# Mixture of experts on one core: tokens turned ahead of the first product, the list of further blocks moved behind the last expert

## The chip, the core and the metric

The kernel runs on one core of a Trainium2 chip. Its engines are TensorE (PE; its weight loads are shown as PEld), VectorE (DVE), ScalarE (ACT), GpSimd (POOL) and SyncE (SP), each with an instruction stream of its own that runs in order; they wait for each other by semaphores. Sixteen DMA engines move data between HBM and the core's memory. POOL issues the indirect DMAs (gather of rows, scatter with addition); SP issues most others. The metric is the device time of one execution in microseconds, as a median over runs.

## What is computed

One block of a hybrid model on 2048 tokens of width 1024: a token mixer with four branches, then a mixture of 32 experts with two experts for each token, then a norm. Only the experts matter here:

```
def grouped_experts(h, expert_ids, weights, w1, w3, w2):
    # tokens sorted by expert, in blocks; for each block xb of expert e:
    #   out = (silu(xb @ w1[e]) * (xb @ w3[e])) @ w2[e]
    # then out * weight of the token for this expert, summed over the token's two experts

def hier_moe(...):
    # group by argmax of group logits, then the two best experts of the group
x = x + m_l[5] * y_l.reshape(x.shape)
return rms_norm(x, final_norm_w)
```

An expert has w1 and w3 of 1024x512 and w2 of 512x1024, in float32: 6.3 MB for each, and all 32 are read.

## The kernel before

The mixer and the router fill the first 2205 us or so. Then come the experts, one after another, and behind them the final norm. The change lies in `ffn`, in the part from line 796 on.

**One expert.** The router has left a list of token rows for each expert, up to 192 of them in two parts: a first block of 128, and a rest of up to 64 in two blocks of 32 that stand behind guards (`tc.If` on the expert's count). `gather` (line 846) fetches the rows with an indirect DMA into one of two tiles, `xg` of 128 rows or `xg` of 64 rows; there is one buffer of each, and the 1025th column of a row is the token's weight for this expert. `turn` (880) turns the 128 rows: eight transposes on PE in two halves of four, each half into a PSUM bank `ps_tr` (there are two such banks, which all transposes share), and `parts` (864) takes each half out as a rounded high part (`xh`, ScalarE cast, line 869) and the remainder (`xl`, VectorE, line 870). `turn` also copies the weight column into `w0` (884). `turn_rest` does it for the 64 rows, in full precision (`xq`, and four small copies into `w1`). `up` (895) is the first product: 48 matmuls with 512 columns, three for each pair of parts (lines 1368 to 1370), against w1 and w3, then silu on ScalarE (903) and the gate on VectorE (904), which multiplies by `w0`; its result `mh0` is turned like `xg` into `hh` and `hl`. `down` (918) is the second product with 24 matmuls, a product with `m5` on VectorE (921), and `added`, the scatter onto the rows of X1 in HBM (908), one tile `my0`. The rest blocks have the same steps in `up_rest`, `gate_rest` (`mh1`, turned into `hq`) and `down_rest`, and use 32-column tiles of PE.

**Weights.** `unit` (800) loads 512 KB into a tile `mraw` (pool of `RAW` = 16), then `split` makes the rounded part `mhi` (ScalarE cast, line 1224) and the remainder `mlo` (VectorE, line 1225), pools of `PARTS` = 12 each. An expert has twelve units: four each for w1, w3 and w2. The rest blocks read `mraw` itself.

**The loop** (from line 1018) writes, for expert e: `up_rest(e)`, the gate of the rest, `up(e)`, the turning of `mh1`, then `turn(e+1)` and `turn_rest(e+1)`, the two gathers of expert e+2, the weights w1 and w3 of e+1, `down(e-1)`, the weights w2 of e, `down_rest(e)` and the turning of `mh0`. A scheduler then sets the final order on each engine; what the program says is only its input. Buffers are freed and taken by semaphores between the engines.

**The list of further blocks.** `beyond` (972) works out on VectorE which experts have more than 192 tokens, as a list `ovt`, `ovf` for a loop behind all experts, whose count is read by `values_load`. It stands behind expert 4. Its tile `le` has the tag of `mh1` and so shares its one buffer.

**The end.** Behind the loop over further blocks, X1 is loaded in 16 tiles, some of which take over slots of `mraw` and the others slots of `mhi` and `mlo`; each is squared, normed and stored.

Of the kernel before, what the change touches and what calls it, by code (L numbers as in the profile page):

```python
# [4 lines left out]
F32 = mybir.dt.float32  # L5
F32R = mybir.dt.float32r
# [555 lines left out]
NE, FF = 32, 512  # L562
# [1 line left out]
NSLOT = 2  # L564
FIT = 192
NONE = 1 << 20
RAW, PARTS = 16, 12
OVB = 32


def ffn(tc, G, A, out, bcast, rsqrt, split, mm3, MT, MR, X1, FR, mid):
# [9 lines left out]
    hl = rp.tile([128, 2, 2, N], BF, name="hl")  # L581
# [23 lines left out]
    with tc.tile_pool(reuse_waits="tile", name="wo", bufs=1, side="right") as wop, \  # L605
# [5 lines left out]
        y0, w1 = [mid.part(0, k) for k in range(4)], mid.kept(1)  # L611
# [195 lines left out]
    wp = mo.enter_context(tc.tile_pool(reuse_waits="tile", name="mo", bufs=1))  # L807
# [39 lines left out]
    def gather(idx_ap, half, guard):  # L847
        xg = xgs[half]
        with guard():
            nc.gpsimd.indirect_dma_start(out=xg, out_offset=None, in_=FR,  # L850
                                         in_offset=bass.IndirectOffsetOnAxis(ap=idx_ap, axis=0),
                                         bounds_check=2 * T - 1, oob_is_err=False)
        return xg

    def turned_into(put, src, r, n, w=128):

        for c in range(0, n, 512 // r):
            m = min(n - c, 512 // r)
            pt = psum("tr")
            for k in range(m):  # L860
                nc.tensor.transpose(pt[:, k * r:(k + 1) * r], src[:, (c + k) * 128:(c + k + 1) * 128], G.ident[:r, :r])
            put(slice(c, c + m), pt[:, :m * r].rearrange("p (k t) -> p k t", t=r))

    def parts(src, n, name):

        hi, lo = (wp.tile([128, n, 128], F32R, name=name + c) for c in "hl")

        def put(c, v):
            nc.scalar.copy(hi[:, c], v)
            nc.vector.tensor_sub(lo[:, c], v, hi[:, c].bitcast(F32))  # L870
        turned_into(put, src, 128, n)
        return hi, lo

    def plain(src, n, name):

        t = wp.tile([128, n, 64], F32, name=name)
        turned_into(lambda c, v: nc.scalar.copy(t[:, c], v), src, 64, n)
        return t

    def turn(xg):  # L880

        p = parts(xg, 8, "x")
        w = wp.tile([128, 1], F32, name="w0", bufs=2)
        nc.scalar.copy(w, xg[:, D:D + 1])
        return p, w

    def turn_rest(xg):

        p = plain(xg, 8, "xq")
        w = wp.tile([64, 2], F32, name="w1", bufs=2)  # L890
        for j, h in product(range(2), range(2)):
            nc.scalar.copy(w[h * 32:h * 32 + 32, j:j + 1], xg[j * 32:j * 32 + 32, D:D + 1])
        return p, w

    def up(xw, w1, w3):

        x, w = xw
        pa = [psum("mm"), psum("mm")]
        for p, ws in zip(pa, (w1, w3)):
            mm3(p, lambda k: (x[0][:, k], x[1][:, k]),  # L900
                lambda k: tuple(t[:, (k % 2) * 512:(k % 2) * 512 + 512] for t in ws[k // 2][:2]), range(8))
        h = wp.tile([128, FF], F32, name="mh0")
        nc.scalar.activation(h, pa[0], AF.Silu)
        nc.vector.scalar_tensor_tensor(h, pa[1], w, h, op0=OP.mult, op1=OP.mult)
        return h
# [8 lines left out]
    def down(h, w2, dst, rest=()):  # L914

        y = wp.tile([128, D], F32, name="my0")
        py = [psum("sc"), psum("sc")]
        for c, (p, ws) in enumerate(zip(py, w2)):
            o = slice(512 * c, 512 * c + 512)
            mm3(p, lambda k: (h[0][:, k], h[1][:, k]), lambda k: tuple(t[:, o] for t in ws[k][:2]), range(4))  # L920
            nc.vector.tensor_mul(y[:, o], p, m5[:, o])  # L921
        added(y, dst, X1, rest)


    def quarters(p, n, guard, x, ws):

        def block(j):
            with guard(j):  # L928
                for k, g in product(range(n), range(4)):
                    nc.tensor.matmul(p[g * 32:g * 32 + 32, j * 256:j * 256 + 256], x(k, j), ws(k, g),  # L930
                                     start=k == 0, stop=k == n - 1)
                if not j:
                    block(1)
        block(0)

    def up_rest(xw, w1, w3, guard):

        w = [w1, w3]
        quarters(hu, 8, guard, lambda k, j: xw[0][:, k, j * 32:j * 32 + 32],
                 lambda k, g: w[g // 2][k // 2][2][:, (k % 2) * 512 + (g % 2) * 256:][:, 0:256])  # L940

    def gate_rest(xw):
        h = wp.tile([64, FF], F32, name="mh1")
        nc.scalar.activation(h, hu[0:64], AF.Silu)
        for j in range(2):
            o = slice(j * 256, j * 256 + 256)
            nc.vector.scalar_tensor_tensor(h[:, o], h[:, o], xw[1][:, j:j + 1], hu[64:128, o], op0=OP.mult, op1=OP.mult)
        return h
# [17 lines left out]
    def in_weights(e_, q=nc.sync, eng=lambda n, u: nc.vector):  # L966
        f2 = lambda n, u: A[n][e_][:, 2 * u:2 * u + 2].rearrange("p k n -> p (k n)")
        return [[unit(f2(n, u), q, eng(n, u)) for u in range(4)] for n in ("e1", "e3")]
# [33 lines left out]
    def fetch(e_, guard):  # L1002
        return gather(idx[:, e_:e_ + 1], 0, nullcontext), gather(idx[0:64, NE + e_:NE + e_ + 1], 1, guard)
# [3 lines left out]
    over = lambda big: lambda j: tc.If(big > 128 + 32 * j)  # L1007
    guards = [over(load(e_)) for e_ in range(2)]
    rows_ = fetch(0, nullcontext)
    x = turn(rows_[0]), turn_rest(rows_[1])  # L1010
    rows_ = fetch(1, lambda: guards[1](0))
    sct4 = wr.tile([128, NE, 2], I32, name="sct4")
    for g, j in product(range(4), range(2)):
        nc.gpsimd.tensor_scalar(sct4[g * 32:g * 32 + 32, :, j], sct[j * 32:j * 32 + 32, NE:], 4.0, float(g), op0=OP.mult, op1=OP.add)
    with tc.issue_after(listed.ins):
        w13 = in_weights(0, eng=lambda n, u: nc.gpsimd if n == "e1" and u < 2 else nc.vector)
    last = None
    for e_ in range(NE + 1):
        if e_ < NE:
            guard = guards[e_]  # L1020
            if e_ + 2 < NE:
                guards.append(over(load(e_ + 2)))

            up_rest(x[1], *w13, guard)
            h1 = gate_rest(x[1])
            h = up(x[0], *w13)
            t1 = plain(h1, 4, "hq")
            q = nc.sync if e_ else nc.gpsimd
            if e_ + 1 < NE:
                x = turn(rows_[0]), turn_rest(rows_[1])  # L1030
                if e_ + 2 < NE:
                    rows_ = fetch(e_ + 2, lambda: guards[e_ + 2](0))
                w13 = in_weights(e_ + 1, q)
        if last:
            down(last[0], [last[1]] * 2, sct[:, e_ - 1:e_], last[2])
        if e_ < NE:
            w2 = [unit(A["e2"][e_][:, u], q) for u in range(4)]
            rest = down_rest(t1, w2, guard, e_)
            last = parts(h, 4, "h"), w2, rest
            if e_ == 4:  # L1040
                beyond()


# [8 lines left out]
    with tc.For_i(0, nov, 1) as it:  # L1052
        ee = nc.values_load(ovt[0:1, bass.ds(it, 1)], min_val=0, max_val=NE - 1)
        sb = wp.tile([128, 1], F32, name="ovb")
        nc.vector.tensor_copy(sb, ovf[:, bass.ds(it, 1)])
        pb = psum("sc")
        for k in range(2):
            dlt = wp.tile([128, N], F32, name="ovd")
            nc.vector.tensor_scalar(dlt, slot[k], sb, None, op0=OP.subtract)
            for i in range(N):  # L1060
                P = wp.tile([128, 128], BF, name="ovP")
                for c in range(4):
                    nc.vector.tensor_scalar(P[:, c * 32:(c + 1) * 32], i32_, dlt[:, i:i + 1], float(-c * 32),
                                            op0=OP.subtract, op1=OP.is_equal)
                nc.tensor.matmul(pb[:, 0:2], P, hl[:, k, :, i], start=k + i == 0, stop=k == 1 and i == N - 1)
        tv = wp.tile([128, 2], F32, name="ovv")
        nc.vector.tensor_scalar(tv[:, 0:1], pb[:, 0:1], 64.0, -64.0, op0=OP.mult, op1=OP.add)
        nc.vector.tensor_add(tv[:, 0:1], tv[:, 0:1], pb[:, 1:2])
        ix = wp.tile([128, 1], I32, name="ovix")
        ixs = wp.tile([128, 1], I32, name="ovixs")  # L1070
        assign(ix, ixs, tv[:, 0:1], tv[:, 1:2], own[:, 0:1])
        dy = lambda n: A[n][bass.ds(ee, 1)].rearrange("e p k n -> (e p) k n")
        f2 = lambda n, u: dy(n)[:, 2 * u:2 * u + 2].rearrange("p k n -> p (k n)")
        w1, w3 = (InTurn(lambda u, n=n: f2(n, u), otiles) for n in ("e1", "e3"))
        w2 = [InTurn(lambda u: dy("e2")[:, u], otiles) for _ in range(2)]
        h = up(turn(gather(ix, 0, nullcontext)), w1, w3)
        down(parts(h, 4, "h"), w2, ixs)


# [512 lines left out]
```

## Time and profile before

| | us |
|---|---|
| median of three runs | 3152.03 (3132.4 to 3156.81) |
| the profiled execution | 3149.57 |
| its span, first to last instruction | 3147.7 |
| TensorE busy in it | 2852.9 (91%) |
| loop over experts, about | 2235 to 3095 |
| mean granted clock of TensorE | 0.953 of full speed |

The profile page gives one execution: busy time of each engine, a timeline in 40 slices, the DMA queues and the costliest groups of instructions. The views of the trace give single instructions with their start, how long the engine stood idle before each, and which instruction let it go. "PEq" is PE's own sequencer (branches and registers). The granted clock is the share of TensorE's full clock that it was given in a stretch.

### The profile page before, as it was taken

How to read it: one execution, taken by the hardware profiler on the slowest of the kernel's cores; microseconds unless marked ns; L12 is line 12 of the kernel's file. 1: busy time of each engine (PE TensorE's matmuls, PEld its weight loads, DVE VectorE, ACT ScalarE, POOL GpSimd, SP SyncE). 2: the span in 40 equal slices, each digit the busy share in tenths (PEclk: the TensorE clock that was granted, in tenths of full speed). 3: DMA queues.
4: the chain of work that ended last, by engine and by line, in shares of the span. 5: the costliest groups of instructions: out<-in, count | busy, mean ns of one | idle time of the engine just before them, and what ended most of it. 6: DMA issues, size and time to landing. Idle time of an engine off the chain costs nothing. (4 is left out here: it accounts for less than half of the span.)

```text
span 3147.7 us, 43618 instructions
## 1 busy us (share of the span) xinstructions
PE 2852.9 (91%) x15893; PEld 2229.4 (71%) x15893; DVE 1827.1 (58%) x2870; ACT 1160.4 (37%) x1722; POOL 583.6 (19%) x522
## 2 busy tenths in 40 slices
PE   7998999999867999899999999999588998999992
PEld 3887887777655677677777777888466676666662
DVE  4624125978776587433334334566678677777674
ACT  5411122322345032232223212322466566666552
POOL 3300010000014021013334333000211212112211
PEclk8999999999978899999999999999798999999996
DMA  7636244423128376765436434554788788888876
GB/s 295 243 111 210 87 158 154 144 81 110 52 72 277 124 225 202 254 237 194 134 120 207 131 125 149 187 169 148 268 292 276 262 300 279 303 289 286 273 235 238
DMA packets 245984, 621.48 MB, mean 197 GB/s; under 512 B 31128, under 2 KB 81464, under 8 KB 242008
## 3 DMA queue, kind: packets, MB, share of 16 engines
q1 hardware_dynamic: 211312, 506.17, 46.6%
q0 software_dynamic: 34416, 111.88, 12.4%
q8 instruction: 163, 2.67, 0.3%
q14 instruction: 93, 0.76, 0.1%
HBM read 484.86 MB, written 137.28 MB: 198 GB/s over the span
## 5 line engine op out<-in xcount | busy, mean ns | idle before, releaser
L1225 DVE TENSOR_TENSOR mlo<-mraw,mhi 128x1024 fp32r<-128x1024 f32 x382 | 447.8, 1225 | 61.4 <-ACT mhi L1224 61.3
L1224 ACT CAST mhi<-mraw 128x1024 fp32r<-128x1024 f32 x384 | 382.5, 1046 | 53.9 <-PE ps_mm L1370 16.1
L1368 PE MATMUL ps_mm<-hb1h,wlo 128*128 128x512 f32 x800 | 319.9, 400 | 2.6 <-DVE wlo L1225 2.6
L1369 PE MATMUL ps_mm<-hb1l,whi 128*128 128x512 f32 x800 | 317.9, 397 | 0.0
L1370 PE MATMUL ps_mm<-hb1h,whi 128*128 128x512 f32 x800 | 317.8, 397 | 0.0
L1519 ACT ACTIVATE ev<-ps_mm 128x512 f32<-128x512 f32 x128 | 76.3, 598 | 612.1 <-PE ps_mm L1370 511.5
L1225 DVE TENSOR_TENSOR wlo<-wraw,whi 128x1024 fp32r<-128x1024 f32 x164 | 214.9, 1319 | 145.1 <-ACT whi L1224 145.0
L1368 PE MATMUL ps_mm<-hb0h,wlo 128*128 128x512 f32 x672 | 270.0, 402 | 16.0 <-DVE wlo L1225 12.5
L1369 PE MATMUL ps_mm<-hb0l,whi 128*128 128x512 f32 x672 | 269.7, 401 | 0.0
L1370 PE MATMUL ps_mm<-hb0h,whi 128*128 128x512 f32 x672 | 267.9, 399 | 0.0
L1224 ACT CAST whi<-wraw 128x1024 fp32r<-128x1024 f32 x176 | 182.1, 1045 | 169.2 <-PE ps_mm L1370 69.8
L1569 POOL TENSOR_TENSOR macc<-macc,ev 128x512 f32<-128x512 f32 x96 | 165.8, 1727 | 309.0 <-DVE ev L1568 306.2
L1568 DVE TENSOR_TENSOR ev<-ev,ps_tr 128x512 f32<-128x512 f32 x96 | 65.8, 687 | 249.9 <-PE ps_tr L1370 243.4
L1369 PE MATMUL ps_mm<-mlo,xh 128*128 128x512 f32 x512 | 203.7, 398 | 6.9 <-PEq L928 3.0
L1368 PE MATMUL ps_mm<-mhi,xl 128*128 128x512 f32 x512 | 206.2, 403 | 1.8 <-ACT mhi L1224 1.4
L1370 PE MATMUL ps_mm<-mhi,xh 128*128 128x512 f32 x512 | 202.9, 396 | 2.5 <-PEq L928 2.2
L908 POOL DMA_INDIRECT d_X<-my,sct x51 | 100.7, 1974 | 444.6 <-DVE my L921 289.6
L1368 PEld LDWEIGHTS ps_mm<-hb1h,wlo 128*128 128x128 f32 x800 | 151.3, 189 | 37.0 <-issue 3.4
L1370 PEld LDWEIGHTS ps_mm<-hb1h,whi 128*128 128x128 f32 x800 | 151.2, 189 | 33.0 <-issue 2.4
L1369 PEld LDWEIGHTS ps_mm<-hb1l,whi 128*128 128x128 f32 x800 | 151.3, 189 | 32.2 <-issue 1.9
L1368 PEld LDWEIGHTS ps_mm<-hb0h,wlo 128*128 128x128 f32 x672 | 128.0, 191 | 45.9 <-DVE wlo L1225 14.3
L1369 PEld LDWEIGHTS ps_mm<-hb0l,whi 128*128 128x128 f32 x672 | 128.1, 191 | 29.3 <-issue 3.2
(588 smaller groups left out, 5898.7 us busy)
## 6 DMA issues: line engine op xcount, KB each, us to landing
mraw<-e SPq DMA_DIRECT2D x372, 512.0 KB
wraw<-wg SPq DMA_DIRECT2D x80, 512.0 KB
wraw<-wt SPq DMA_DIRECT2D x40, 512.0 KB
aw<-adaw SPq DMA_DIRECT2D x64, 256.0 KB
d_GS<-ev SPq DMA_DIRECT2D x64, 256.0 KB
ev<-d_GS POOLq DMA_DIRECT2D x64, 256.0 KB, 4.4
wraw<-wg POOLq DMA_DIRECT2D x24, 512.0 KB, 4.3
d_FR<-hb0h SPq DMA_DIRECT2D x22, 512.0 KB
```

What stands on the lines that cost most here:

```text
L908: d = nc.gpsimd.indirect_dma_start(out=out, out_offset=bass.IndirectOffsetOnAxis(ap=dst, axis=0), in_=y, in_offset=None, compute_op=OP.add)
L1224: nc.scalar.copy(hi, raw)
L1225: eng.tensor_sub(lo, raw, hi.bitcast(F32))
L1368: nc.tensor.matmul(ps, wl, xh, start=start and n == 0, stop=False)
L1369: nc.tensor.matmul(ps, wh, xl, start=False, stop=False)
L1370: nc.tensor.matmul(ps, wh, xh, start=False, stop=stop and n == len(ks) - 1)
L1519: nc.scalar.activation(g, ps, AF.Sigmoid)
L1568: nc.vector.tensor_mul(g, g, ps)
L1569: nc.gpsimd.tensor_add(acc, acc, g)
```

## The change

Four things change.

1. `turn(e+1)` is written ahead of `up(e)`, and `xh` and `xl` have two buffers instead of one. The copy of the weight column leaves `turn` and becomes `weights`, which stays where it was.
2. `w0` and `w1` have one buffer each instead of two.
3. `RAW` is 14 instead of 16, so two more of the final norm's tiles lie in slots of `mhi` and `mlo`.
4. `beyond()` is called behind the last expert instead of behind expert 4.

```
-RAW, PARTS = 16, 12
+RAW, PARTS = 14, 12

-    def parts(src, n, name):
-        hi, lo = (wp.tile([128, n, 128], F32R, name=name + c) for c in "hl")
+    def parts(src, n, name, bufs=1):
+        hi, lo = (wp.tile([128, n, 128], F32R, name=name + c, bufs=bufs) for c in "hl")

     def turn(xg):
-        p = parts(xg, 8, "x")
-        w = wp.tile([128, 1], F32, name="w0", bufs=2)
+        return parts(xg, 8, "x", 2)
+
+    def weights(xg):
+        w = wp.tile([128, 1], F32, name="w0")
         nc.scalar.copy(w, xg[:, D:D + 1])
-        return p, w
+        return w

     def turn_rest(xg):
         p = plain(xg, 8, "xq")
-        w = wp.tile([64, 2], F32, name="w1", bufs=2)
+        w = wp.tile([64, 2], F32, name="w1")

-    x = turn(rows_[0]), turn_rest(rows_[1])
+    x = turn(rows_[0]), weights(rows_[0]), turn_rest(rows_[1])

-            up_rest(x[1], *w13, guard)
-            h1 = gate_rest(x[1])
-            h = up(x[0], *w13)
+            up_rest(x[2], *w13, guard)
+            h1 = gate_rest(x[2])
+            nx = turn(rows_[0]) if e_ + 1 < NE else None
+            h = up(x[:2], *w13)
             t1 = plain(h1, 4, "hq")
             q = nc.sync if e_ else nc.gpsimd
             if e_ + 1 < NE:
-                x = turn(rows_[0]), turn_rest(rows_[1])
+                x = nx, weights(rows_[0]), turn_rest(rows_[1])

-            if e_ == 4:
+            if e_ == NE - 1:
                 beyond()
```

The order of instructions on the engines moves more than these lines show. Lines of the changed kernel are higher by 1 in `ffn` behind `turn`, and by 3 in `split` and the matmul helper.

First place: PE around the second half of expert 12's work. Of the names, `xg_16950` is the tile of 128 gathered rows, `xg_16951` that of 64, `ps_mm` belongs to `up`, `ps_sc` to `down`, and `mh_21167` is `mh1` of expert 12. Before, from the last matmul of `up(12)` on:

```order
L1370 MATMUL ps_mm<-mhi,xh 128x512
L861 MATMUL ps_tr<-c_kid,mh_21167 128x64 x4
L861 MATMUL ps_tr<-c_kid,xg_16950 128x128 x4
L1368 MATMUL ps_sc<-mhi,hl 128x512
L1369 MATMUL ps_sc<-mlo,hh 128x512
L1370 MATMUL ps_sc<-mhi,hh 128x512
L1368 MATMUL ps_sc<-mhi,hl 128x512
L861 MATMUL ps_tr<-c_kid,xg_16950 128x128 x4
L1369 MATMUL ps_sc<-mlo,hh 128x512
L1370 MATMUL ps_sc<-mhi,hh 128x512
L1368 MATMUL ps_sc<-mhi,hl 128x512
L861 MATMUL ps_tr<-c_kid,xg_16951 128x64 x8
```

Now, PE ahead of `up(12)`; `mh_20872` is `mh0` of expert 11, and the `ps_mm` rows are the first of `up(12)`:

```order
L1371 MATMUL ps_sc<-mhi,hl 128x512
L1372 MATMUL ps_sc<-mlo,hh 128x512
L1373 MATMUL ps_sc<-mhi,hh 128x512
L861 MATMUL ps_tr<-c_kid,mh_20872 128x128 x4
L861 MATMUL ps_tr<-c_kid,xg_16950 128x128 x4
L1371 MATMUL ps_mm<-mhi,xl 128x512
L1372 MATMUL ps_mm<-mlo,xh 128x512
L929 COMPARE_AND_BRANCH
L931 MATMUL ps_hf_16946<-mraw,xq 32x256 x32
```

And now, PE behind the last matmul of `up(12)`, where the branch is the end of a guard and `mh_21135` is `mh1` of expert 12:

```order
L960 UNCONDITIONAL_BRANCH x4
L861 MATMUL ps_tr<-c_kid,xg_16950 128x128 x4
L1371 MATMUL ps_sc<-mhi,hl 128x512
L1372 MATMUL ps_sc<-mlo,hh 128x512
L1373 MATMUL ps_sc<-mhi,hh 128x512
L1371 MATMUL ps_sc<-mhi,hl 128x512
L1372 MATMUL ps_sc<-mlo,hh 128x512
L861 MATMUL ps_tr<-c_kid,mh_21135 128x64 x4
L1373 MATMUL ps_sc<-mhi,hh 128x512
```

The first half of the transposes of expert 13's tokens moved from behind `up(12)` to ahead of it, and the second half from behind the transposes of `mh1` to ahead of them; `up_rest(12)` now stands among the first matmuls of `up(12)`.

Second place: ScalarE beside it. `xq` and `hq` are the copies of turned rest tokens and of turned `mh1`, `w_21247` is `w0` of expert 13, `w_20882` and `w_20895` are `w0` and `w1` of expert 12. Before, from `hh` of expert 11 to `xq` of expert 13:

```order
L869 CAST hh<-ps_tr 128x512
L884 COPY w_21247<-xg_16950 128x1
L1224 CAST mhi<-mraw 128x1024 x3
L903 ACTIVATE mh_21221<-ps_mm 128x512
L1224 CAST mhi<-mraw 128x1024 x2
L959 UNCONDITIONAL_BRANCH
L1224 CAST mhi<-mraw 128x1024 x3
L877 COPY hq<-ps_tr 128x256
L869 CAST xh<-ps_tr 128x512 x2
L849 UNCONDITIONAL_BRANCH
L877 COPY xq<-ps_tr 128x512
```

Now, from the second half of `xh` of expert 12 to the first half of `xh` of expert 13:

```order
L869 CAST xh<-ps_tr 128x512
L893 COPY w_20895<-xg_16951 32x1 x4
L1227 CAST mhi<-mraw 128x1024
L877 COPY hq<-ps_tr 128x256
L885 COPY w_20882<-xg_16950 128x1
L1227 CAST mhi<-mraw 128x1024
L849 UNCONDITIONAL_BRANCH
L877 COPY xq<-ps_tr 128x512
L1227 CAST mhi<-mraw 128x1024 x2
L869 CAST hh<-ps_tr 128x512
L869 CAST xh<-ps_tr 128x512
```

The copy `w0` moved behind `hq`, and both `xh` halves are apart. At each expert between none and two casts stand between the second `xh` and `w0` (here one).

Third place: VectorE at the end of the loop. `my_27617` and `my_27585` are the product of the rest of expert 31, `my_27632` in both is the output of `down(31)`. Before:

```order
L955 TENSOR_TENSOR my_27617<-ps_hf_16947,m5x 128x512
L870 TENSOR_TENSOR hl<-ps_tr,hh 128x512
L959 UNCONDITIONAL_BRANCH
L921 TENSOR_TENSOR my_27632<-ps_sc,m_16956 128x512 x2
L1051 TENSOR_LOAD ovt
```

Now, from the last step of the running sums on (the comparison and the ten small operations ahead of it stand behind `hl`):

```order
L988 TENSOR_TENSOR inc_27618<-inc_27615 128x16
L990 TENSOR_TENSOR le<-inc_27618,i__14714 128x1024
L999 CAST ovt<-inc_27618 128x1
L922 TENSOR_TENSOR my_27632<-ps_sc,m_16956 128x512
L993 TENSOR_REDUCE ej<-le 128x32
L994 TENSOR_TENSOR le<-le,ov 128x1024
L998 CAST ovt<-ej 128x32
L922 TENSOR_TENSOR my_27632<-ps_sc,m_16956 128x512
L996 TENSOR_REDUCE bj<-le 128x32
L1000 TENSOR_SCALAR ej<-ej 128x32
L997 TENSOR_TENSOR bj<-i__14714,bj 128x32
L1001 SCALAR_TENSOR_TENSOR ovf<-bj,ej 128x32
```

The list's operations stand around the two products of `down(31)`; in the kernel before they stand around weight subtractions, as the trace shows.

## Rows read from the trace of the kernel before

**Rows 1.** The page, busy time: engine, us, share of span, instructions.

```profile
PE 2852.9 (91%) x15893; PEld 2229.4 (71%) x15893; DVE 1827.1 (58%) x2870; ACT 1160.4 (37%) x1722; POOL 583.6 (19%) x522
```

**Rows 2.** Busy time by stretch: length, each engine's, then granted clock, DMA share, GB/s.

```profile
2420.00:2740.00 320.00, 297.98 (x2012) 219.54 (x2010) 230.63 (x255) 196.57 (x295) 65.77 (x40) 0.96 0.85 286
2400.00:2410.00 10.00, 9.53 (x34) 7.06 (x35) 8.35 (x11) 4.97 (x11) 1.07 (x1) 0.55 0.97 265
```

**Rows 3.** By line, 2420 to 3050 us: busy us, mean ns; idle before, releasers.

```profile
L1224 ACT CAST mhi<-mraw 128x1024 fp32r<-128x1024 f32 x287 | 285.4, 1046 | 40.1 <-PE ps_mm L1370 14.2 <-PE ps_sc L1370 13.5 <-issue 7.6
...
L861 PE MATMUL ps_tr<-c_kid,xg 128*128 128x128 f32 (+1 forms) x380 | 54.2, 271 | 20.9 <-ACT hq L877 20.6
```

**Rows 4.** Timeline, waits for `hq`: start us, us, engine, line [idle before, releaser].

```profile
2442.97 1.07 PE L861 MATMUL ps_tr<-c_kid,xg 128*128 128x128 f32 x4 [3.36 <-ACT hq L877]
...
2778.15 4.82 ACT L1224 CAST mhi<-mraw 128x1024 fp32r<-128x1024 f32 x5
...
2782.87 0.36 ACT L877 COPY hq<-ps_tr 128x256 f32<-128x256 f32 x1
2783.14 0.59 ACT L869 CAST xh<-ps_tr 128x512 fp32r<-128x512 f32 x1
...
2783.29 1.11 PE L861 MATMUL ps_tr<-c_kid,xg 128*128 128x128 f32 x4 [3.96 <-ACT hq L877]
...
2785.17 1.04 POOL L850 DMA_INDIRECT xg<-d_FR,idx  x1 [13.34 <-ACT xh L869]
```

**Rows 5.** Busy time by stretch, PE alone: busy, granted clock, DMA share, GB/s.

```profile
2783.20:2787.00 3.80, 3.71 (x11) 0.50 0.32 124
```

**Rows 6.** Timeline of VectorE, ScalarE and PE around the list of further blocks.

```profile
2380.26 0.65 DVE L980 TENSOR_TENSOR le<-cnt,thr 128x480 bf16<-128x480 f32 x1
...
2389.69 1.22 DVE L989 TENSOR_TENSOR le<-inc,i__14714 128x1024 bf16<-128x1024 f32 x1
...
2396.10 1.21 DVE L995 TENSOR_REDUCE bj<-le 128x32 f32<-128x1024 bf16 x1
...
2397.34 0.59 ACT L944 ACTIVATE mh<-ps_hf 64x512 f32<-64x512 f32 x1 [7.64 <-DVE bj L995]
...
2398.66 0.47 PE L861 MATMUL ps_tr<-c_kid,mh 64*128 64x64 f32 x2 [10.78 <-DVE mh L947]
```

**Rows 7.** Timeline of VectorE and POOL at the end of the loop.

```profile
3087.49 0.68 DVE L870 TENSOR_TENSOR hl<-ps_tr,hh 128x512 fp32r<-128x512 f32 x1
3093.27 1.53 DVE L921 TENSOR_TENSOR my<-ps_sc,m 128x512 f32<-128x512 f32 x2 [5.10 <-DMA d_X<-my,sct]
...
3093.93 1.55 POOL L908 DMA_INDIRECT d_X<-my,sct  x1 [5.12 <-DMA d_X<-my,sct]
3095.79 1.55 POOL L908 DMA_INDIRECT d_X<-my,sct  x1 [0.30 <-issue]
```

**Rows 8.** Instructions on tile `xg`: ns min/median/max; landing of the gathers.

```profile
L850 POOL DMA_INDIRECT xg<-d_FR,idx x48: 943/1130/2052, 2226.5 to 3029.8; - x48
...
L884 ACT COPY w<-xg x32: 188/191/194, 2235.1 to 3041.5; 128x1 f32<-128x1 f32 x32
...
DMA to landing us min/median/max: 3.0/5.4/10.6
```

**Rows 9.** Timeline of PE at full clock: transposes and two successive matmuls.

```profile
2622.23 0.46 PE L861 MATMUL ps_tr<-c_kid,mh 64*128 64x64 f32 x4
...
2623.34 0.39 PE L1369 MATMUL ps_sc<-mlo,hh 128*128 128x512 f32 x1
2623.57 0.39 PE L1370 MATMUL ps_sc<-mhi,hh 128*128 128x512 f32 x1
...
2624.04 0.60 PE L861 MATMUL ps_tr<-c_kid,xg 128*128 128x128 f32 x4
...
2625.50 0.71 PE L861 MATMUL ps_tr<-c_kid,xg 64*128 64x64 f32 x8
```

**Rows 10.** Timeline of PE, an early expert's second product.

```profile
2304.47 0.77 PE L1368 MATMUL ps_sc<-mhi,hl 128*128 128x512 f32 x1 [4.97 <-DVE hl L870]
```

More of the change, by code (lines that the diff above doesn't have):

```diff
@@ L1075, in ffn @@
         w2 = [InTurn(lambda u: dy("e2")[:, u], otiles) for _ in range(2)]
-        h = up(turn(gather(ix, 0, nullcontext)), w1, w3)
+        xg = gather(ix, 0, nullcontext)
+        h = up((turn(xg), weights(xg)), w1, w3)
         down(parts(h, 4, "h"), w2, ixs)
```

## Prediction

> **What bounds the kernel now.** I read the page first: TensorE is busy 91% of the span, VectorE 58%, ScalarE 37% [rows 1]. The change touches only the loop over experts and the few microseconds behind it, so I then read busy time by stretch. In 2420 to 2740 us PE is busy 298.0 of 320.0 us at a granted clock of 0.96, with the DMA engines at 0.85 [rows 2]. So PE bounds the loop, and DMA stands close behind it: what PE wins comes to the end almost in full, unless DMA is pushed over its limit. Next I looked for what PE waits for there. Grouped by line over 2420 to 3050 us, the transposes of gathered tokens (line 861, `xg`) wait 20.6 us in eight waits, for ScalarE's copy `hq` [rows 3]. The timeline shows one of the eight: five weight casts stand ahead of `hq` on ScalarE from 2778.15 on, `hq` runs only at 2782.87, and the next transposes, which need the PSUM bank that `hq` empties, have waited 3.96 us [rows 4]. The granted clock behind that wait is 0.50 for 3.8 us, the lower of the two levels (1.2 against 2.4 GHz) [rows 5]. The single longest wait in the loop is another: 10.78 us at 2398.66, and the clock of 2400 to 2410 is 0.55 [rows 2, 6].
>
> **Part 1, the list of further blocks.** It now comes behind expert 31 and not behind expert 4. In the loop its VectorE work begins at 2380.26 and ends with a reduction at 2396.10 (weight subtractions stand in between). Its tile `le` shares a slot with `mh1`, so ScalarE's `mh1` waits 7.64 us for that reduction, and PE's transposes of it start 10.78 us late [rows 6]. Without the list these transposes should come like any others, with a gap of perhaps 0.4 us: 10.4 us less. The lost clock behind it is 10 us x (1 - 0.55) = 4.5 us, and I count 5 with the 1.3 us before that stretch. Together **-15.4 us**.
>
> At the tail the list is not free. VectorE ends `hl` at 3088.17 and then idles 5.10 us until the scatter of expert 30 lets go of `my0`; two products with `m5` take 1.53 us and end at 3094.80; the last scatter starts at 3095.79, because another one occupies POOL from 3093.93 [rows 7]. By the new order (third place shown) the list up to the second `le` stands ahead of the first product: about 4.3 us by the durations in its old place, so it fits the 5.10 us. Between the two products stand a reduction, a product of 128x1024 and a cast, 1.21 (its like, `bj`) + 1.22 (its like, the first `le`) + 0.2 - overlap = 2.4 us [rows 6]. The second product ends near 3097.1 and the last scatter starts about 1.4 us later than now. The rest of the list (about 1.6 us) runs beside that scatter. **+1.4 us**. Bounds: 0, and +4 if the first half doesn't fit the idle time.
>
> **Part 2, the `hq` waits.** In the new PE order all eight transposes of `xg` no longer stand on both sides of the transposes of `mh1`: half of them come ahead of `up`, half right behind it, and what then needs the bank of `hq` is `mh0`, 17 matmuls of `down` later (17 x 0.23 = 3.9 us, and `xgrest` besides). That is longer than the casts that remain ahead of `hq` (0 to 2 at 1.05 us instead of up to 5). So the 20.6 us go, and with them the clock: six of the eight waits (3.36, 0.91, 0.17, 2.80, 1.91, 3.96, 3.96 and 3.54 us; the first and the sixth have their rows) are of 1.9 us or more [rows 4], and the stretch that I read lost 3.8 x 0.5 = 1.9 us [rows 5], so 6 x 2 = 12 us. **-33 us**. Upper end of it: none of it, if `hq` stays late (a rival).
>
> **Part 3, what is late next: the gather.** There is one tile `xg`. The gather for expert e+2 may start only when all transposes of e+1 have read it and ScalarE has copied `w0` out of it. That copy now has one buffer, which the gate of expert e must have left. Before, the gathered rows were needed one `up` and one `down` later; POOL's wait of 13.34 us at 2785.17 costs nothing there [rows 4]. Now the first half of those rows is needed ahead of the next `up`, so the cover of `up` (48 x 0.23 = 11 us) is gone, and one `down` has to hide copy, gather and landing. With T the end of `up`: on ScalarE transposes 0.60, `xh` 0.59, four `w1` copies and `w0` at 0.19 (0.95), `hq` 0.37, n casts at 1.05, on POOL 0.3 to the issue: the gather starts at T + 2.8 + 1.05n [rows 3, 4, 7 to 9]. PE comes to the next `xg` transposes after transposes 0.60, 24 matmuls at 0.23 (5.5), `mh1` 0.46, `xgrest` 0.71, `mh0` 0.60: T + 7.9 [rows 9]. With a landing of L the wait is L + 1.05n - 5.1.
>
> The order of ScalarE gives n = 2 for experts 4, 5, 6, 8, 14, 15, 16, n = 1 for 12 and 13, n = 0 for 7, 9, 10, 11; from 17 on matmuls of `up` and a rest block or its guard stand ahead of the transposes, so I count little for these. L is 3.0 at least, 5.4 in the median, 10.6 at most [rows 8]. The median includes gathers beside the full burst of weights at the loop's start, so I take 5.0: 2.0 us for seven experts, 0.95 for two, together 16; the clock behind about half of the seven, 7 us; and 2 us for all from 17 on. **+25 us**. Bounds: 0 at L = 3.0, since 3.0 + 2.1 - 5.1 = 0, and about +92 at L = 6.5 (worked out as a rival).
>
> The Trainium skill has a price for such a transfer in "DMA: Bandwidth & Descriptors", section "Anatomy of one DMA — SWDGE (gpsimd) path": about 2.0 us and the bytes at 436 GB/s. For 128 rows of 4.1 KB this makes an estimate of 3.2 us, and the wait at n = 2 would be 0.2 us: by this rule the whole term goes. The trace disagrees, with its median of 5.4 us beside weight traffic, and my sum goes by the trace.
>
> **Part 4, the rest.** `w1` in one buffer is written behind the gate of the rest block, long done. The second `x` buffer is what lets transposes precede `up`; it adds no instruction. Two raw buffers fewer: the twelve units of 512 KB of an expert still fit into 14, but the first burst of weights is two units shorter. In the first experts a late `hl` costs PE 4.97 us once [rows 10], and the new order puts `hh` and `hl` earlier against `down`, so it may go. I set burst against `hl`: **-1 us**, bounds -7 and +5. The guards are as many as before, and what PE waits at them stays.
>
> **Sum** on the profiled execution's 3149.6 us: -15.4 + 1.4 - 33 + 25 - 1 = -23, so **3126.6 us**. The median of the three runs is 3152.0, 2.5 us above the profiled one; a measurement of this kernel can tell about 1% (31.5 us) from no change, so faster means below 3120.5 and slower above 3183.5.
>
> **Rivals.**
> - *The gather is hidden after all* (L near 4): the 25 us fall to 0 to 3, and the time is 3102 to 3105. For it: the traffic of weights pauses after `down_rest` frees raw buffers late, and an idle DMA lands a gather in 3.0 us [rows 8]. It is also where the Trainium skill's 3.2 us would lead. Against it: DMA share 0.85.
> - *The `hq` waits only move*, since the same casts stand on the same ScalarE and now hold up `xh` of the second half or `hh`: part 2 falls to a third (-11), the gather costs 10, and 3149.6 - 14 - 11 + 10 - 1 = 3134 us; with a little more of either, 3140 to 3150.
> - *The gather is late at every expert* (slower). Place: the transposes ahead of `up`. At L = 6.5 an expert with n = 2 waits 3.5 us and loses 2 of clock: 7 x 5.5 + 2 x 4.5 + 4 x 1.4 = 53, and 14 experts from 17 on at 2.8 each = 39: +92, and 3149.6 - 48 + 92 = 3194 us. It decides from L = 5.6 on, where the waits eat all of the gain, and L = 6.3 makes more than 1%. For it: the median is 5.4. Against: most of the loop's late gathers run beside less traffic than the early ones.
> - *Raw buffers*: with 14, two units (1 MB) less are under way when `up_rest` or `down_rest` releases late; at DMA share 0.85 this could cost 0.5 us for each of 31 experts, and 3126.6 + 15 = 3142.
>
> **Chances.** Forecast as told (3112 to 3136) 0.37; hidden gather (3095 to 3112) 0.2; moved `hq` waits or raw buffers (3136 to 3160) 0.27; late gather (above 3160) 0.16, of which 0.13 above 3183. Below 3120.5 lie the hidden gather and half of the forecast: faster 0.38; same 0.49; slower 0.13. The range leaves out less than 0.1 at each end: 3098 to 3175; the likeliest case alone is 3112 to 3136.
>
> **What would show it.** Part 1: no PE wait above 4 us near the sixth expert, clock near 0.95 in the window behind it, the last scatter 1 to 2 us later after `hl`. Part 2: no PE wait for `hq` in the waits by line. Part 3: PE waits at line 861 released by the gather's DMA, 1 to 2.5 us each at experts 4 to 16, few behind 17, some with 0.50 of clock behind. The landing of the gathers decides: a median above 5.6 us makes the prediction wrong to the slow side, one near 4 to the fast side. Part 4: PE waits for `mlo` or `mhi` in the loop would tell of raw buffers.

## The result: slower by half a per cent, and the profile after

The changed kernel takes 3167.11 us against 3150.86 us, medians of ten runs each. The ratio is 1.0054 (95% interval 1.0028 to 1.008), 17 us more, where the prediction had 23 us less. The time lies within the stated range, but on the other side of no change.

The page of the changed kernel, busy times; the span answers to the table of before, the engines to [rows 1]:

```profile
span 3158.6 us, 43403 instructions
...
PE 2846.5 (90%) x15893; PEld 2227.7 (71%) x15893; DVE 1830.1 (58%) x2870; ACT 1150.7 (36%) x1722; POOL 594.9 (19%) x522
```

The spans differ by 11 us only, because this execution was 14 us faster in the unchanged stages before the experts (its first gather starts at 2212.56, that of before at 2226.52). From the first gather to the end it takes 946.0 us where before took 921.2: 25 us more in these two executions.

Busy time by stretch, the columns as in [rows 2]:

```profile
2420.00:2740.00 320.00, 283.36 (x1899) 204.77 (x1898) 214.02 (x234) 177.27 (x267) 61.48 (x37) 0.94 0.77 261
2740.00:3050.00 310.00, 284.82 (x1913) 210.07 (x1912) 228.94 (x252) 188.63 (x287) 74.36 (x39) 0.97 0.87 290
```

In the first stretch PE lost 14.6 us of busy time and the DMA engines are less busy, so there nothing came closer to its limit; PE waits. By line, 2420 to 3050 us, as in [rows 3]:

```profile
L1227 ACT CAST mhi<-mraw 128x1024 fp32r<-128x1024 f32 x278 | 276.6, 1048 | 0.5
...
L861 PE MATMUL ps_tr<-c_kid,xg 128*128 128x128 f32 (+1 forms) x368 | 47.2, 260 | 49.3 <-DMA xg<-d_FR,idx 48.2 <-PEq L929 1.0
...
L893 ACT COPY w<-xg 32x1 f32<-32x1 f32 x92 | 17.4, 189 | 0.9
```

The 20.6 us for `hq` are gone. In their place PE waits 48.2 us for the landing of the gather. Waits of 2260 to 3050 us (in total, times, longest):

```profile
PE ps_tr L861 <- DMA xg<-d_FR,idx: 63.7, 21, 11.8
```

Over the whole loop, behind its first gather, it is 67.8 us in 23 waits, and PE stands idle for 101.1 us where it was 79.5 before.

One of these waits, at the gather of expert 9's rows (timeline of ScalarE, POOL and PE):

```profile
2433.12 1.05 ACT L1227 CAST mhi<-mraw 128x1024 fp32r<-128x1024 f32 x1
...
2434.07 0.36 ACT L877 COPY hq<-ps_tr 128x256 f32<-128x256 f32 x1
2434.34 1.05 ACT L1227 CAST mhi<-mraw 128x1024 fp32r<-128x1024 f32 x1
2435.28 0.19 ACT L885 COPY w<-xg 128x1 f32<-128x1 f32 x1
...
2435.44 1.46 POOL L850 DMA_INDIRECT xg<-d_FR,idx  x1 [13.58 <-ACT mhi L1227]
...
2445.07 1.09 PE L861 MATMUL ps_tr<-c_kid,xg 128*128 128x128 f32 x4 [5.58 <-DMA xg<-d_FR,idx]
```

Two casts and `hq` stand ahead of `w0`, as the order said, and the gather starts as soon as `w0` ends. But 9.63 us pass until PE goes on. The windows around it (PE busy, granted clock, DMA share, GB/s):

```profile
2428.00:2435.40 7.40, 7.40 (x42) 1.00 1.03 360
2435.40:2439.40 4.00, 4.00 (x20) 1.00 1.02 408
2439.40:2444.60 5.20, 0.09 (x1) 0.87 0.57 211
2444.60:2450.00 5.40, 4.93 (x32) 0.50 0.00 0
```

The gather is issued into a DMA share of 1.02, and PE starves from 2439.4 on. When PE goes on, DMA is at 0.00: no weight load moves any more. Behind these 5.6 us of idling the clock is 0.50, the lower of its two levels, for the next 5.4 us. Whether the weight loads delayed the gather, `a_half` tests.

### The profile page after: what moved, and what is told of

Same layout as the page of the kernel before. It is cut to its first block, busy times and chain, and to the rows that moved or that the text cites. A ratio compares the mean times of both kernels' runs of the same rounds, so it can differ in the third digit from the quotient of the medians.

```text
span 3158.6 us, 43403 instructions
## 1 busy us (share of the span) xinstructions
PE 2846.5 (90%) x15893; PEld 2227.7 (71%) x15893; DVE 1830.1 (58%) x2870; ACT 1150.7 (36%) x1722; POOL 594.9 (19%) x522
## 5 line engine op out<-in xcount | busy, mean ns | idle before, releaser
L1371 PE MATMUL ps_mm<-mhi,xl 128*128 128x512 f32 x512 | 214.7, 419 | 10.5 <-PEq L929 8.8
L1372 PE MATMUL ps_mm<-mlo,xh 128*128 128x512 f32 x512 | 213.4, 417 | 5.3 <-PEq L929 2.7
L1373 PE MATMUL ps_mm<-mhi,xh 128*128 128x512 f32 x512 | 211.2, 413 | 2.9 <-PEq L929 1.8
```

The costliest lines, as they stand in the source:

```text
L1371: nc.tensor.matmul(ps, wl, xh, start=start and n == 0, stop=False)
L1372: nc.tensor.matmul(ps, wh, xl, start=False, stop=False)
L1373: nc.tensor.matmul(ps, wh, xh, start=False, stop=stop and n == len(ks) - 1)
```

## The experiments

**The parts of the change, one at a time on the kernel before.** First the list alone:

```
-            if e_ == 4:
+            if e_ == NE - 1:
                 beyond()
```

> The kernel before with the list of further blocks behind the last expert, nothing else. By the prediction's part 1 the wait of 10.78 us and the slow clock behind it go (-15.4 us) and the tail costs 1.4 us: ratio 0.9955, and no PE wait above 5 us around the sixth expert. Rival: the 10.8 us only gave the weights time to come, and the next expert waits for them instead: ratio 1.0.

Measured: 0.9952 (0.9935 to 0.997), about 15 us, as part 1 forecast. That the number fits so well is in part luck. The order of the whole loop changed too: the waits for `hq` (20.6 us before) are gone in this run, and a new wait took their place (2260 to 3050 us: in total, times, longest):

```profile
PE ps_sc L1368 <- DVE hl L870: 30.0, 10, 7.2
```

The raw buffers alone (`RAW` 16 to 14):

> The kernel before with 14 raw buffers instead of 16, nothing else. Theory G: no change beyond noise, ratio 0.998 to 1.002, no new waits for mhi or mlo on TensorE. Rival R (the raw buffers were worth 0.5 us for each expert): about 15 us more, ratio 1.005, with waits of ScalarE's casts for the loads.

Measured: 0.9936 (0.9913 to 0.9958), faster by 20 us, which neither theory had. The waits of that run:

```profile
PE ps_tr L861 <- ACT hq L877: 12.3, 4, 4.8
```

They were 20.6 us in eight. In the order of ScalarE 13 of 32 experts now have three or four casts directly ahead of `hq` instead of five. That a smaller pool itself is worth something isn't shown; see `b_w_list`.

**The gather.** In `x2` the gathered rows have two tiles in turn:

```
+    xg2 = wr.tile([128, D + 1], F32, name="xg2")
...
+        if half == 0:
+            xg = (xg, xg2)[turnof[0] % 2]
+            turnof[0] += 1
```

> The changed kernel with two tiles of 128 gathered rows in turn instead of one (three small tiles of the list of further blocks share slots, to make room), so that a gather no longer has to wait for the transposes and the w0 copy of the expert before it. Theory G (the changed kernel loses because the gather came onto TensorE's path): waits of TensorE for the gather fall from 68 us in the loop to under 10 us, no waits for hq come back, and the time is that of before less what the list and the hq waits cost there: 3151 - 15 - 33 + 2 = about 3105 us, ratio to before 0.98 to 0.99. Rival M (the new order or the 14 raw buffers cost the time, the gather waits only stand where another wait would): other waits take the place, and the time stays at 3150 us or above, ratio 1.0 or more.

Measured: 0.9763 (0.9741 to 0.9785), 3083.81 us, and behind the loop's first gather the trace shows not one wait of TensorE for a gather or for `hq` (for two waits at the transposes, of 4.7 and 1.4 us, it shows no releaser). So the gather is what the changed kernel lost by, and theory G stands. But the gain exceeds the 48 us that the prediction's other parts add up to by 27 us: something else in the change was worth more than I had given it.

`a_w0_early` copies `w0` beside the early transposes, in two buffers (part of the edit):

```
-            nx = turn(rows_[0]) if e_ + 1 < NE else None
+            nx = (turn(rows_[0]), weights(rows_[0])) if e_ + 1 < NE else None
```

> The changed kernel with the w0 copy written beside the early transposes again, in two buffers, and nothing else. Theory G: on ScalarE the copy no longer stands behind casts and hq, so the gather is issued up to 2.5 us sooner at experts with two casts and 0.5 us sooner at those with none; the gather waits fall by some 1.5 us each at 24 places, 68 to about 35 us, and the time to about 3167 - 35 - 8 (clock) = 3125 us, ratio to before 0.99. If the landing is set by the weight traffic and not by the issue (rival T), the gathers land at the same places, the waits stay above 55 us, and the time stays within 5 us of the changed kernel, ratio 1.004.

Measured: 0.998 (0.9957 to 1.0002), about 23 us faster than the changed kernel, about half of what was expected. Its waits of 2260 to 3050 us:

```profile
ACT w L885 <- DMA xg<-d_FR,idx: 129.5, 27, 14.4
PE ps_tr L861 <- DMA xg<-d_FR,idx: 43.6, 18, 11.6
```

TensorE's 63.7 us in that stretch fell to 43.6, but ScalarE now stands 129.5 us at the early copy, behind which its casts wait. ScalarE copies one column only, but it waits for the whole gather, and all that stands behind the copy waits too.

`a_half` and `b_half` load half of each unit (the first line of the edit):

```
-        q.dma_start(raw, src)
+        q.dma_start(raw[:, 0:512], src[:, 0:512])
```

> The changed kernel with half of each weight unit loaded: each load brings 512 of the 1024 columns (256 KB), and casts, subtractions and the rest blocks read these columns twice, so that TensorE, ScalarE and VectorE have as much to do as before; the products are of the wrong weights. Theory T (the gathers land late because weight traffic shares the DMA engines): the gathers land 4 to 5 us after their issue instead of 7 to 8 at the middle experts, TensorE's waits for them fall from 68 to under 25 us. Rival D (POOL's descriptors or its queue take the time): landing stays at 6 us or more, the waits above 50 us.

> The kernel before with half of each weight unit loaded in the same way, as the measure of what less traffic brings by itself. Theory T: TensorE is the bound in the loop and the gathers are hidden there, so the loop of 859 us becomes shorter by less than 15 us, and a_half comes out shorter than b_half. If the loop were bound by DMA, it would fall by 50 us or more.

Landing of the gathers, in `b_half` (to be held against 5.4 us in [rows 8]), in the changed kernel and in `a_half`; last, the wait of PE for them in `a_half`, 2420 to 3050 us:

```profile
DMA to landing us min/median/max: 3.6/4.7/9.1
...
DMA to landing us min/median/max: 3.8/6.2/8.3
...
DMA to landing us min/median/max: 3.4/5.1/14.0
...
PE ps_tr L862 <- DMA xg<-d_FR,idx: 49.1, 11, 7.0
```

With half the traffic the median landing falls from 5.4 to 4.7 us in the kernel before, where the traces tell all 48 gathers, and from 6.2 to 5.1 us in the changed one, where they tell 11 and 43 of 48. The gathers of experts 3, 6 and 8 took 4.8, 4.7 and 4.8 us, and none of experts 6 to 11 makes PE wait. So traffic does lengthen the landing. The expected fall of the waits did not come. In this run's order `w0` ends 4 to 7.5 us behind the transposes from expert 14 on instead of at most 3.7 us, and some gathers start later still: from expert 15 on 6.0 us behind the transposes in the median, 4.0 in the changed kernel. The run is confounded there and decides only on the landing. `b_half` ran 12 us shorter in the loop (846.7 against 858.9), so DMA was not the bound before, as the prediction had read.

**Whether the early turn is worth anything.** In `x2_late_turn` the two tiles stay and the turn goes back behind `up`; `a_late_turn` is the same edit on the changed kernel with its one tile:

```
-            nx = turn(rows_[0]) if e_ + 1 < NE else None
             h = up(x[:2], *w13)
             t1 = plain(h1, 4, "hq")
+            nx = turn(rows_[0]) if e_ + 1 < NE else None
```

> The kernel with two gather tiles, with the turning of the next expert's tokens written behind the first product again (in place of ahead of it), all else as there: list behind the last expert, 14 raw buffers, one buffer for w0 and w1. It gives the worth of the early turn by itself once the gather is out of the way. By the prediction's part 2 the early turn is worth 33 us: about 3084 + 33 = 3117 us, ratio to before 0.987, with waits for hq of 10 to 20 us. Rival (the early turn is worth nothing, list and raw buffers brought all of it): ratio 0.976 to 0.980, no such waits.

> The changed kernel with the turning of the next expert's tokens written behind the first product again: list behind the last expert, 14 raw buffers and single w0 and w1 as in the change, one gather tile. Theory S: the list and the raw buffers keep their gain (0.9952 and 0.9936 alone), the gather leaves TensorE's path and goes back to ScalarE's: ratio 0.988 to 0.993, no gather waits of TensorE, ScalarE waiting for the gather for 60 us or more; so the early turn with one tile costs 1.2 to 1.8%. Rival: single w0 and w1 buffers cost it: ratio 1.0 or more.

`x2_late_turn`: 0.9782 (0.9752 to 0.9811), against 0.9763: the early turn brings nothing that can be measured, even where its gather is hidden, and there are no waits for `hq` without it either. My part 2 falls. `a_late_turn`: 0.9755 (0.9732 to 0.9778), 3084.34 us: with one gather tile, undoing the early turn makes the changed kernel 3% faster, far more than list and raw buffers had shown, and faster than before by 2.4%. By line, 2420 to 3050 us:

```profile
L861 PE MATMUL ps_tr<-c_kid,xg 128*128 128x128 f32 (+1 forms) x368 | 50.4, 258 | 0.0
...
L893 ACT COPY w<-xg 32x1 f32<-32x1 f32 x92 | 17.4, 190 | 9.7 <-issue 5.1 <-ACT mhi L1227 2.1 <-DMA xg<-d_FR,idx 1.5
```

No wait of TensorE at the transposes, and ScalarE waits 1.5 us for the gather: it did not go back to ScalarE, which theory S said.

`b_x2` gives the kernel before two gather tiles, as `x2` does:

> The kernel before with two tiles of 128 gathered rows in turn instead of one (three small tiles of the list share slots, to make room) and nothing else: 16 raw buffers, list behind expert 4, tokens turned behind the first product. Theory S (the single gather tile already bound the loop before, on ScalarE: its copies of w0 and w1 wait for the landing, 92 us in 20 waits, and the casts queued behind them pile up ahead of hq): those waits fall under 20 us, the waits of TensorE for hq fall from 20.6 to under 5 us, and the time is near that of x2_late_turn with the list's 15 us on top, ratio 0.98 to 0.985. Rival (the gather was hidden before, and the gain of x2 comes from the 14 raw buffers, the single w buffers or the list): ratio 0.995 to 1.0.

Measured: 0.9997 (0.9984 to 1.0011). Its waits of 2260 to 3050 us:

```profile
ACT w L898 <- DMA xg<-d_FR,idx: 93.9, 17, 14.1
...
PE ps_tr L867 <- ACT hq L883: 22.9, 8, 3.9
```

A second tile does nothing there, and theory S as I had put it falls: ScalarE waits for gathers as before, at the copies of `w1`, whose tile of 64 rows was not doubled, and TensorE for `hq`. What remains of the change are the single buffers of `w0` and `w1`. `x2_w2` takes them back in `x2` (`bufs=2` for both):

> The kernel with two gather tiles and the early turn, with two buffers for w0 and w1 again. Theory S: the single buffers cost nothing once the tile is doubled: ratio 0.974 to 0.979, like x2. Rival (they hold ScalarE until the gate is done): 5 us or more faster than x2, ratio below 0.974.

Measured: 0.9873 (0.9854 to 0.9891), slower than `x2` by 1.1%, 34 us, which neither theory had. The wait is back:

```profile
ACT w L899 <- DMA xg<-d_FR,idx: 104.9, 16, 16.1
...
PE ps_tr L867 <- DVE hl L876: 17.1, 6, 5.2
```

**The single buffers alone.** In the kernel before, `bufs=2` is taken from `w0` and `w1` (`b_w`), or from `w1` only (`b_w1`); `b_w_list` is `b_w` with the list behind the last expert (the edit for `w1`):

```
-            w = wp.tile([64, 2], F32, name="w1", bufs=2)
+            w = wp.tile([64, 2], F32, name="w1")
```

> The kernel before with w0 and w1 in one buffer each, and nothing else (list behind expert 4, 16 raw buffers, one gather tile, late turn). Theory W (with two buffers the copies of w1 for the next expert stand on ScalarE right behind xq and wait there for a gather that can start only when xq has been read; one buffer puts them back behind the gate): ScalarE's waits for the gather fall from 92 us to under 15 us, TensorE's for hq from 20.6 to under 10 us, ratio 0.982 to 0.990 (a_late_turn's 0.9755 without the list's 0.9952 and at least half of the raw buffers' 0.9936). Rival (the gain needs the three parts together): ratio above 0.995.

> The kernel before with only w1 in one buffer; w0 keeps two. Theory W: w1 is the one that matters (77 us of the 92 in before stand at its line): same as b_w within 0.3%. Rival (w0 matters too): half of b_w's gain or less.

> The kernel before with w0 and w1 in one buffer each and the list behind the last expert; 16 raw buffers, late turn: what is left of the change without the early turn and without the smaller raw pool. Theory W: list and single buffers make the gain and the raw buffers only shuffled the order: ratio 0.972 to 0.980, as a_late_turn. Rival R (14 raw buffers are worth 0.6% by themselves): ratio 0.980 to 0.985.

Measured: `b_w` 0.9842 (0.9826 to 0.9859), `b_w1` 0.9863 (0.9846 to 0.988), `b_w_list` 0.9779 (0.9762 to 0.9796). Theory W stands: one buffer less for each of two tiles of 4 and 8 bytes a row makes the kernel 50 us faster, and 43 of that come with `w1` alone. The cause can be seen in the kernel before (timeline of ScalarE, POOL and PE, expert 17):

```profile
2683.20 0.59 ACT L877 COPY xq<-ps_tr 128x512 f32<-128x512 f32 x1 [1.26 <-PE ps_tr L861]
2690.93 0.39 ACT L892 COPY w<-xg 32x1 f32<-32x1 f32 x2 [7.14 <-DMA xg<-d_FR,idx]
...
2692.38 3.89 ACT L1224 CAST mhi<-mraw 128x1024 fp32r<-128x1024 f32 x4
...
2700.07 4.83 ACT L1224 CAST mhi<-mraw 128x1024 fp32r<-128x1024 f32 x5
2704.80 0.37 ACT L877 COPY hq<-ps_tr 128x256 f32<-128x256 f32 x1
...
2683.85 1.89 POOL L850 DMA_INDIRECT xg<-d_FR,idx  x1 [0.71 <-ACT xq L877]
...
2705.22 0.66 PE L861 MATMUL ps_tr<-c_kid,xg 128*128 128x128 f32 x4 [1.91 <-ACT hq L877]
```

The copy of the next `w1` stands right behind `xq`. It needs the next gather into the tile of 64 rows, which POOL starts only behind `xq`, so ScalarE stands there for issue and landing, 7.14 us. The casts behind it come late and then fill the time ahead of `hq`, for which TensorE waits. With one buffer the copy has to wait for the gate of the expert at hand, and in the order of `b_w` it stands around the next `hq`, when the rows are long there (timeline of ScalarE, `b_w`, expert 17):

```profile
2678.89 0.59 ACT L892 COPY w<-xg 32x1 f32<-32x1 f32 x3
2679.39 0.37 ACT L877 COPY hq<-ps_tr 128x256 f32<-128x256 f32 x1
```

By line, 2420 to 3050 us, the kernel before and then `b_w`:

```profile
L892 ACT COPY w<-xg 32x1 f32<-32x1 f32 x96 | 18.2, 190 | 82.7 <-DMA xg<-d_FR,idx 70.1 <-DVE mlo L1225 11.4
```

```profile
L861 PE MATMUL ps_tr<-c_kid,xg 128*128 128x128 f32 (+1 forms) x384 | 51.0, 257 | 0.3 <-PEq L928 0.2
...
L892 ACT COPY w<-xg 32x1 f32<-32x1 f32 x93 | 17.5, 189 | 1.0
```

Over the loop (858.9 to 811.5 us) TensorE's idle time falls by 27.7 us, 20.1 of it waits for `hq` and 7.3 for `hl`, and its work by 19.7 us, at a mean granted clock of 0.966 where it was 0.943.

Where ScalarE's standing still hits TensorE depends on the order. In `b_list_last` ScalarE waited for gathers even longer than before (139.8 us in 34 waits, 92.5 in 20 before), and TensorE waited not for `hq` but for `hl`. The longest of these waits (timeline of ScalarE and PE, `b_list_last`) stands behind a copy of `w0` that held up the casts:

```profile
3001.59 0.19 ACT L884 COPY w<-xg 128x1 f32<-128x1 f32 x1 [12.14 <-DMA xg<-d_FR,idx]
...
3003.54 0.58 ACT L869 CAST hh<-ps_tr 128x512 fp32r<-128x512 f32 x1
...
3010.07 0.77 PE L1368 MATMUL ps_sc<-mhi,hl 128*128 128x512 f32 x1 [7.23 <-DVE hl L870]
```

**The sum, from the runs** (each part added to the ones above it, us at 3151):

| parts | ratio to before | step |
|---|---|---|
| one buffer for `w0` and `w1` (`b_w`) | 0.9842 | -50 |
| and the list behind the last expert (`b_w_list`) | 0.9779 | -20 |
| and 14 raw buffers, second `x` buffer (`a_late_turn`) | 0.9755 | -8 |
| and the early turn: the changed kernel | 1.0054 | +94 |
| and two gather tiles (`x2`) | 0.9763 | -92 |

Each ratio is known to some 5 to 8 us. `a_late_turn` and `x2` both beat both kernels, by 2.4% over the kernel before.

## Why the prediction was wrong, step by step

**Part 1, the list: right.** -14 forecast with the tail, -15 alone and -20 on top of the single buffers. Alone, the wait of 10.78 us went as forecast, and that all else came out near nothing is luck: waits for `hq` of 20.6 us went and those for `hl` rose by 23. On top of the single buffers neither moves. The tail costs a little more than 1.4 us (timeline of VectorE and POOL, changed kernel, against [rows 7]):

```profile
3096.01 0.68 DVE L870 TENSOR_TENSOR hl<-ps_tr,hh 128x512 fp32r<-128x512 f32 x1
...
3102.56 0.69 DVE L922 TENSOR_TENSOR my<-ps_sc,m 128x512 f32<-128x512 f32 x1 [1.84 <-DMA d_X<-my,sct]
...
3105.64 0.68 DVE L922 TENSOR_TENSOR my<-ps_sc,m 128x512 f32<-128x512 f32 x1
...
3106.60 1.57 POOL L909 DMA_INDIRECT d_X<-my,sct  x1 [1.79 <-DVE my L922]
```

From the start of `hl` to the last scatter it is 10.6 us against 8.3, so +2.3; 0.8 of that is a later landing of the scatter before. The first half of the list fits the idle time, as forecast.

**Part 2, the `hq` waits: gone as forecast, but the early turn is worth nothing by it.** -33 forecast; with two gather tiles the early turn brings 6 us (0.9782 to 0.9763), less than the intervals can tell. The single buffers alone take the waits away (0.5 us left in `b_w`), so the gain is theirs. Where `w1` has two buffers (`x2_w2`), the early turn removes the waits for `hq` too, but 17.1 us for `hl` stand at the same transposes: the rival that the waits only move. I followed the chain from TensorE one step, to the five casts ahead of `hq`, and stopped at their number. In the case shown they ran that late because ScalarE had stood still behind `w1`. The waits by line would have shown it: 70.1 us at line 892. I had left idle time of ScalarE out, since it is busy for 37% only [rows 1].

**Part 4, one buffer for `w1`, put at nothing: the largest gain, 50 us with `w0`.** The step asked when the copy is written, and found the gate long done. It did not ask where the copy stands in the order with two buffers, and what it waits for there. The claim of part 3 that gathered rows were needed an `up` and a `down` later, and that the gather cost nothing before, fails with it: it held for the transposes, not for ScalarE's copies.

**Part 3, the gather: right mechanism, sized at 25 us, measured 94.** The formula for its start was good: 3.7 us from the transposes to the end of `w0` at two casts, and PE at the next transposes 7.5 us behind; it gives L - 3.5 where the prediction had L - 3.0. Three terms were too small. The landing: 5.0 taken; from issue to TensorE's going on it was 7.3 us in the median of the 20 gathers from expert 4 on that it waited for. These are the late ones; of the 11 gathers whose landing the trace tells it is 6.2, still above the 5.6 that the prediction had named as the sign of a miss to the slow side. The experts from 17 on: 2 us taken; 22.8 us measured, of which 11.78 us at expert 30, whose gather stood 4.6 us behind two scatters on POOL besides (timeline of POOL and PE, changed kernel):

```profile
3005.19 2.45 POOL L909 DMA_INDIRECT d_X<-my,sct  x1 [8.87 <-DVE mlo L1228]
3007.95 1.96 POOL L909 DMA_INDIRECT d_X<-my,sct  x1 [0.30 <-issue]
3010.21 1.41 POOL L850 DMA_INDIRECT xg<-d_FR,idx  x1 [0.30 <-issue]
...
3021.77 1.09 PE L861 MATMUL ps_tr<-c_kid,xg 128*128 128x128 f32 x4 [11.78 <-DMA xg<-d_FR,idx]
```

The first three experts behind the loop's first, which I had left out: 7.0 us. With 38.0 us at experts 4 to 16 (16 in the prediction) this makes 67.8 us. The rest of the 94 is slow clock and other waits: against `a_late_turn` TensorE is idle for 69 us more (101.1 and 31.7) and its work takes 25 us longer (780.2 and 755.1). The rival of the late gather said 5.5 us for each expert with two casts and +92 in all; it gave 3194 us, with 33 for the `hq` waits and nothing for part 4. The measured 3167 lies below because the single buffers brought 50 us in place of those 33, and list and raw buffers 13 more than forecast. The rule of the Trainium skill ("DMA: Bandwidth & Descriptors", "Anatomy of one DMA — SWDGE (gpsimd) path") with its estimate of 3.2 us is further off than the median of before; of the 31 gathers into the tile of 128 rows behind the first, in the kernel before, the fastest took 3.96 us.

**Part 4, raw buffers: -1 forecast, -20 alone and -8 on top of the rest** (the intervals of `b_w_list` and `a_late_turn` overlap). In these two runs ScalarE and TensorE do their work in the same order, so a gain of the smaller pool by itself is not shown; the 20 us of `b_raw14` came with another order of the loop. Why that order is faster stays open beyond its shorter waits for `hq`.

The chances put 0.13 on slower by more than 1% and 0.49 on no change, which it is by that bound; the sign was wrong. The early turn came out 102 us worse than forecast (69 in the gather, 33 in the `hq` waits), the single buffers 50 us better, list and raw buffers 13 us better; that these leave only 17 us is luck.

## What to carry to other kernels

Follow an in-order engine's wait to its end: a queue of late work ahead of the one awaited is an answer only when it is known why that work is late, and a small copy from a gathered tile can hold a whole engine for the gather. More buffers let a scheduler place a copy earlier, where its data can't be yet; fewer may be faster. A prefetch into a single buffer that is consumed earlier loses the cover that it had, and its transfer should be priced at the traffic of the place where it now starts.

## What was not expected of the hardware

- The gather of expert 9's 128 rows landed in 4.5 us in the kernel before (issued at 2444.83, DMA share 0.51 until it landed); in the changed kernel, issued at 2435.44, it let PE go on after 9.6 us. In the packet records the first row moves 1.99 us behind the issue in the one and 4.36 us in the other. The 128 rows take 2.2 us in the one; in the other they mix with the rows of the gather issued 1.8 us later, and the 134 rows of both take 4.7 us. So the time grew both ahead of the first byte and during the transfer; how much of it the weight loads and how much the second gather brought isn't shown.
- Stages that the change doesn't touch differed by 14 us between the two profiled executions, 11 of them between about 990 and 1065 us. Spans of single executions of this kernel can't be compared over their whole length; the parts from the first gather on can.
